# Feed-forward products of a decoder layer by a Strassen scheme, with the activations between them in DRAM

## The chip, the core and the metric

The kernel runs on one core of a Trainium2 chip. The metric is the device time of one execution in microseconds (us); the median of three runs is given. Matmuls run on TensorE (PE in the profile; PEld is its weight load), elementwise work on VectorE (DVE), ScalarE (ACT) and GpSimd (POOL); SyncE (SP) issues most DMAs.

## The reference

One post-norm layer on x of 1024 tokens by 1024 channels, all in float32:

```python
mixed = jnp.sum(gates * proj, axis=2) @ w_out[l]
x = _layer_norm(ALPHA * x + mixed, ln1_g[l], ln1_b[l])
hid = jax.nn.silu(x @ w_ffn_gate[l]) * (x @ w_ffn_up[l])
x = _layer_norm(ALPHA * x + hid @ w_ffn_down[l], ln2_g[l], ln2_b[l])
```

The three branches that make `proj` (a state-space branch, a gated recurrence and attention) are not touched. `w_ffn_gate` and `w_ffn_up` are 1024 x 2816, `w_ffn_down` is 2816 x 1024; 2816 are 22 blocks of 128.

## The kernel before

Each float32 product is made of three matmuls: every operand is split into a rounded part `hi` and a rest `lo`, and `mm3` (L108) adds hi·hi, hi·lo and lo·hi into one PSUM bank. `split` (L127) makes the parts: a copy on ACT that rounds, and a subtraction on DVE. A matmul has a stationary side of 128x128 and a moving side of 128x512.

The late part begins behind `merge(2)` (L950), which sums the branches into `mixed` and splits it.

- *Output projection.* `mix_out(tb, dh)` (L913) makes a block of 128 tokens by 512 channels with 24 matmuls; there are 16 such blocks, 384 matmuls. Its result is added to the input row (`stt`), `measure` (L894) takes bn_stats, and `norm` (L899) normalizes a block of 128 tokens: aggregate, square root on ACT, two multiplications, a reciprocal, two more.
- *Turning.* `turn_x(tb)` (L928) transposes a normalized block of tokens by 8 matmuls with the identity and splits it into `XH` and `XL`, the moving side of what follows.
- *Gate and up.* For each of 22 blocks `hb`, `hidden` (L967) sums gate and up for both halves of the tokens over 8 blocks of channels: four banks of 24 matmuls. Silu on ACT, the product of both on DVE, then a split.
- *Down.* The blocks `hb` are taken in chunks of three, the last of four (L978 to L980). Behind a chunk all 16 output blocks get its part (L998 to L1004) and are added in SBUF on DVE (L1008). Activations never leave SBUF. In the last chunk every block of tokens is normalized as soon as it is complete (L1012) and stored.

Weights come in 512 KB loads into `ws` (3 buffers), are split into `wh` and `wl` or into pairs of `m`. The late pools are `t` (9 large tiles and a few small ones, left side of SBUF) and `u` (15, right side). The framework's scheduler orders each engine's instructions with a time model; a tile pool makes an instruction wait until its buffer's last reader is done.

## Time and profile before

| | |
|---|---|
| runs shown | 1759.16 us median (1758.62 to 1762.29) |
| the profiled execution's own time | 1758.93 us |
| its span in the profile | 1757.2 us |
| PE busy | 1702.9 us, 97% of the span |
| DVE, ACT, POOL busy | 866.6, 532.5, 215.3 us |
| merge(2) ends, mix_out starts | 919.10 us |
| feed-forward starts | 1013.76 us |
| last matmul starts | 1748.05 us |

The profile is of one execution. The span runs from its first instruction to its last; the time of the run is 1.7 us longer. Starts are counted from the span's start. Matmuls are pipelined, so one matmul's duration (390 to 396 ns) is longer than the distance between two starts; the distance is what counts.

### The profile page before, as it was taken

What the parts mean: (1) busy time and instruction counts of PE and PEld (TensorE: products, weight loads), DVE (VectorE), ACT (ScalarE), POOL (GpSimd) and SP (SyncE); (2) the same over time, 40 slices, a digit from 0 to 9 for tenths busy, and PEclk for the clock granted to TensorE, in tenths of its full rate; (3) what the DMA queues carried; (4) which work ended last, traced back from release to release, by engine and by line L of the source; (5) the groups of instructions that cost most, each with busy time, mean ns of one, the idle gap of its engine ahead of it and who ended that gap; (6) DMA issues with size and microseconds to landing.
All of it is one profiled execution on the core that took longest, in us unless ns stands there. A gap on an engine that the chain in (4) does not pass through costs nothing.

```text
span 1757.2 us, 20254 instructions
## 1 busy us (share of the span) xinstructions
PE 1702.9 (97%) x7878; PEld 1399.6 (80%) x7878; DVE 866.6 (49%) x1648; ACT 532.5 (30%) x867; POOL 215.3 (12%) x285
## 2 busy tenths in 40 slices
PE   8989999999899998999999999999999999999998
PEld 6868877878688887888888888888888888888886
DVE  4756674624553468877486543232232323223238
ACT  4324454434443536552140131120202112020210
POOL 0210434214431021111400000000000000000000
PEclk9999999999899999999999999999999999999999
DMA  5342233233332434356673021120201111020102
GB/s 158 72 103 66 75 88 88 79 83 94 81 87 68 127 104 131 111 171 224 196 237 113 1 84 60 35 68 18 72 28 57 48 48 60 25 72 25 60 1 96
DMA packets 181789, 150.09 MB, mean 85 GB/s; under 512 B 29632, under 2 KB 153660, under 8 KB 181692
## 3 DMA queue, kind: packets, MB, share of 16 engines
q1 hardware_dynamic: 155580, 121.02, 23.7%
q10 hardware_dynamic: 26112, 27.76, 5.2%
q8 instruction: 62, 1.02, 0.2%
q14 instruction: 35, 0.29, 0.1%
HBM read 116.77 MB, written 31.98 MB: 85 GB/s over the span
## 4 chain that ended last, share of the span: by engine, by line
PE 80%; DMA 2%; DVE 2%; ACT 1%; POOL 1%; issue 1%; SPq 0%; ACTq 0%; DVEq 0%; POOLq 0%
PE b L106 49%; PE a L106 28%; PE s L106 1%; DMA nck<-ck_d 1%; PE a L330 1%; POOL s L114 1%; DMA s<-gl_d 1%; DMA nat<-s_c_re 0%; DVE s L114 0%; DVE x L122 0%; DVE wl L114 0%; DVE s L748 0%; DMA ws<-w_in 0%; POOL ndk L290 0%; PE b L933 0%
## 5 line engine op out<-in xcount | busy, mean ns | idle before, releaser
L106 PE MATMUL b<-x,wh 128*128 128x512 f32 x912 | 352.7, 398 | 2.5 <-ACT s L696 1.7
L106 PE MATMUL b<-x,wl 128*128 128x512 f32 x832 | 329.5, 396 | 0.0
L106 PE MATMUL b<-m,wh 128*128 128x512 f32 x784 | 310.4, 396 | 0.0
L114 DVE TENSOR_TENSOR wl<-ws,wh 128x1024 fp32r<-128x1024 f32 x106 | 136.7, 1290 | 142.7 <-ACT wh L128 132.6
L106 PEld LDWEIGHTS b<-x,wh 128*128 128x128 f32 x912 | 173.3, 190 | 37.6 <-ACT s L696 1.8
L128 ACT CAST wh<-ws 128x1024 fp32r<-128x1024 f32 x106 | 111.3, 1050 | 278.2 <-PE b L106 167.1
L106 PEld LDWEIGHTS b<-x,wl 128*128 128x128 f32 x832 | 158.2, 190 | 31.7
L106 PEld LDWEIGHTS b<-m,wh 128*128 128x128 f32 x784 | 149.3, 190 | 28.6 <-issue 0.2
L106 PE MATMUL b<-m,u 128*128 128x512 f32 x564 | 142.6, 396 | 0.0
L106 PE MATMUL a<-m,u 128*128 128x512 f32 x564 | 141.4, 396 | 0.0
L114 DVE TENSOR_TENSOR zs<-zs,a 128x512 f32<-128x512 f32 x44 | 30.3, 688 | 206.5 <-PE a L106 206.5
L106 PEld LDWEIGHTS a<-m,u 128*128 128x128 f32 x564 | 106.1, 188 | 25.5
L106 PEld LDWEIGHTS b<-m,u 128*128 128x128 f32 x564 | 106.0, 188 | 25.4
L106 PE MATMUL b<-u,wh 128*128 128x512 f32 x352 | 111.3, 396 | 0.0
L106 PE MATMUL a<-u,wh 128*128 128x512 f32 x352 | 111.1, 395 | 0.0
L106 PE MATMUL b<-t,wh 128*128 128x512 f32 x352 | 108.8, 390 | 0.0
L106 PE MATMUL a<-t,wh 128*128 128x512 f32 x352 | 108.7, 390 | 0.0
L114 POOL TENSOR_TENSOR s<-s,s 128x1024 f32<-128x1024 f32 (+9 forms) x76 | 78.5, 1034 | 209.1 <-ACT s L751 82.8
L128 ACT CAST m<-ws 128x1024 fp32r<-128x1024 f32 x26 | 27.4, 1055 | 248.1 <-PE a L106 186.7
L106 PEld LDWEIGHTS b<-u,wh 128*128 128x128 f32 x352 | 66.0, 188 | 16.4 <-DVE u L114 0.4
L106 PEld LDWEIGHTS a<-u,wh 128*128 128x128 f32 x352 | 66.0, 188 | 16.0
L106 PEld LDWEIGHTS b<-t,wh 128*128 128x128 f32 x352 | 66.0, 188 | 14.1
(256 smaller groups left out, 2631.8 us busy)
## 6 DMA issues: line engine op xcount, KB each, us to landing
ws<-w_in SPq DMA_DIRECT2D x48, 512.0 KB, 4.3
gate_d<-zs ACTq DMA_DIRECT2D x48, 256.0 KB, 2.1
zs<-gate_d SPq DMA_DIRECT2D x48, 256.0 KB, 3.3
ws<-w_ffn_gate SPq DMA_DIRECT2D x22, 512.0 KB, 3.8
ws<-w_ffn_up SPq DMA_DIRECT2D x22, 512.0 KB, 4.0
ws<-w_ffn_down SPq DMA_DIRECT2D x22, 512.0 KB, 3.2
ws<-w_branch SPq DMA_DIRECT2D x12, 512.0 KB, 5.6
s<-x SPq DMA_DIRECT2D x8, 512.0 KB, 7.1
```

The lines of the kernel that those rows point to most:

```text
L106: PE.matmul(o, a, b, start=first, stop=last)
L114: return e.tensor_tensor(o, a, b, op)
L128: ACT.copy(hi, src)
L330: PE.transpose(ta[:, j, e, :], pts[e][:, (k0 + j) * P : (k0 + j + 1) * P], ident)
```

## The change

*Gate and up.* The product is taken as a 2x2 matrix of quarters on one side (channels in two halves, gate and up as the two columns) and tokens in two halves on the other. A Strassen scheme in Winograd's form makes the four results from 7 products of quarters, 12 matmuls each, where 8 were needed. `turn` makes seven operands of x (`x11`, `x12`, `x22`, `s1` to `s4`) from both halves of the tokens, `sums` makes four sums of the weights of a block on POOL, and the products are combined by DVE additions (`begin`, `upper_gate`, `middle`, the loop). Blocks 0 to 2 take products 1 and 2 ahead of turn 7.

*Down.* The same scheme with pairs of blocks `hb` and halves of the output channels. For that the gated activations go to DRAM (`hid_d`), with their sums (`hids_d`, on POOL in `gated`) and the sums of the weights (`wts_d`, on POOL in `sums_down`). Then, product by product (order 1, 2, 6, 7, 5, 4), 11 steps each, `factors` loads two factors of 256 KB, splits them, and `blocks` runs 12 matmuls into four banks; `after_...` combines the banks with the residual. The factors of product 3 are all loaded and split ahead (22 tiles `p3`), so that it can be made one block of 128 tokens at a time with the normalization behind.

*Layout.* x behind the first normalization goes to DRAM (`x1_d`) and comes back as residual. The late pools are `keep`, `mid`, `right`, later `down`; PSUM is 8 equal banks. Small tiles of 4 bytes become 64, and an unused tile of 96 bytes lies at the right edge: in the built program before, the `u` tiles begin 32 bytes past a multiple of 64, and now every large tile begins on a multiple of 64. From turn 7 on, `pin` keeps DVE's, ACT's and POOL's instructions in the order of the program.

The core of the diff:

```diff
@@ -56,12 +56,16 @@
+    edge = ctx.enter_context(tc.tile_pool(name="edge", bufs=1, side="right"))
+    POOL.memset(edge.tile([P, 24], F32, name="edge"), 0.0)
...
-        "t": ("t", 9), "ln": ("t", 2), "u": ("u", 15),
+
+    LATE = {
+        "ws": ("keep", 4), "w": ("keep", 8), "x": ("keep", 9), "m8": ("mid", 4), "ln": ("mid", 2),
+        "mx": ("right", 8), "wo": ("right", 4), "r": ("down", 8), "row": ("down", 2), "p3": ("down", 22),
+    }
...
+    def pin(ins):
+
+        return tc.keep_in_program_order(ins) if pinned[0] else ins
+
     def tt(e, o, a, b, op):
-        return e.tensor_tensor(o, a, b, op)
+        return pin(e.tensor_tensor(o, a, b, op))
...
+    def operand(n, j, src, e):
+
+        if j == 0:
+            XO[n] = [new(HOME[n], F32R, (P, 4, 512)) for _ in range(2)]
+        hi, lo = [t[:, :, j * P : (j + 1) * P] for t in XO[n]]
+        ACT.copy(hi, src)
+        tt(e, lo, src, hi.bitcast(F32), ALU.subtract)
+
+    def turn(tb, place):
+        j = tb % 4
+        pa = []
         for q in range(2):
-            pa = bank([P, 4, P], "ba"[q])
+            pa.append(place(q))
             for k in range(4):
-                PE.transpose(pa[:, k, :], acc[tb][:, (4 * q + k) * P : (4 * q + k + 1) * P], ident)
...
+                PE.transpose(pa[q][:, k, :], acc[tb][:, (4 * q + k) * P : (4 * q + k + 1) * P], ident)
+        if tb < 4:
+            raw[j] = new("x", shape=(P, 8, P))
+            ACT.copy(raw[j][:, 0:4], pa[0])
+            DVE.tensor_copy(raw[j][:, 4:8], pa[1])
+            operand("x11", j, raw[j][:, 0:4], DVE)
+            operand("x12", j, raw[j][:, 4:8], POOL)
+            return
+        xs, s1 = new("x", shape=(P, 8, P)), new("x", shape=(P, 8, P))[:, 0:4]
+        x22, s2, s3, s4 = xs[:, 0:4], xs[:, 4:8], raw[j][:, 0:4], raw[j][:, 4:8]
+        ACT.copy(x22, pa[1])
+        tt(DVE, s3, s3, pa[0], ALU.subtract)
+        tt(DVE, s1, pa[0], x22, ALU.add)
+        tt(POOL, s2, x22, s3, ALU.subtract)
+        tt(POOL, s4, s4, s2, ALU.subtract)
+        operand("x22", j, x22, DVE)
+        operand("s3", j, s3, DVE)
+        operand("s2", j, s2, POOL)
+        operand("s1", j, s1, DVE)
+        operand("s4", j, s4, POOL)
...
+    def store_parts(hb, src, i, j):
+
+        hi, lo = [new("w", F32R, (P, 8, P)) for _ in range(2)]
+        split(src, hi, lo)
+        WT[hb][i], WT[hb][j] = [[t[:, c] for t in (hi, lo)] for c in (slice(0, 4), slice(4, 8))]
...
+    PRE = 3
+    for hb in range(PRE):
+        store_parts(hb, t, 1, 2)
...
+    def bank8(shape=(P, 512)):
+        return banks.tile(list(shape), F32, name=name("p"), tag="p", bufs=8)
...
+    def product(i, hb):
+        ps = bank8()
+        (wh_, wl_), (xh_, xl_) = WT[hb][i], XO[OF[i]]
+        for k in range(4):
+            mm3(ps, wh_[:, k], wl_[:, k], xh_[:, k], xl_[:, k], k == 0, k == 3)
+        return ps
+
+    def begin(hb):
+        ua, ub = new("x", shape=(P, 2, 512)), new("x", shape=(P, 2, 512))
+        G[hb] = dict(s1=ua[:, 0], u2=ua[:, 1], u3=ub[:, 0], gate=ub[:, 1])
+        pin(ACT.copy(G[hb]["s1"], product(1, hb)))
+
+    def upper_gate(hb):
+        g = G[hb]
+        tt(DVE, g["gate"], g["s1"], product(2, hb), ALU.add)
+        pin(ACT.activation(g["gate"], g["gate"], AF.Silu))
+    for hb in range(PRE):
+        begin(hb)
+        upper_gate(hb)
+    turn(7, lambda q: bank8([P, 4, P]))
+    pinned[0] = True
...
+    def sums(hb):
...
+        tt(POOL, t1, w12, w11, ALU.subtract)
+        tt(POOL, t2, w22, t1, ALU.subtract)
+        tt(POOL, t3, w22, w12, ALU.subtract)
+        tt(POOL, t4, w21, t2, ALU.subtract)
+
...
+    def parts_b(hb):
+        store_parts(hb, RAW[hb, 2][:, 0:8], 5, 6)
+        v = new("x", F32R, (P, 8, P))
+        split(RAW[hb, 1][:, 4:8], v[:, 0:4], v[:, 4:8])
+        WT[hb][3] = [v[:, 0:4], v[:, 4:8]]
+    def parts_c(hb):
+        store_parts(hb, RAW[hb, 2][:, 8:16], 7, 4)
...
+        tt(POOL, w11, w12, w11, ALU.subtract)
+        tt(POOL, w12, w22, w12, ALU.subtract)
+        tt(POOL, w22, w22, w11, ALU.subtract)
+        tt(POOL, w21, w21, w22, ALU.subtract)
+        for e, t in enumerate((wa, wb)):
+            SP.dma_start(wts_d[2 * j + e], t.rearrange("p a b -> p (a b)"))
...
+    def gated(hb):
+
+        g = G[hb]
+        t = hid[hb] = new("ln", shape=(P, 2, 512))
+        tt(POOL, t[:, 1], g["u3"], g["s1"], ALU.mult)
+        tt(POOL, t[:, 0], g["u2"], g["gate"], ALU.mult)
+        SP.dma_start(hid_d[hb], t.rearrange("p a b -> p (a b)"))
+        if hb % 2:
+            (x11, x21), (x12, x22) = [[t[:, 0], t[:, 1]] for t in hid[hb - 1 : hb + 1]]
+            tt(POOL, x11, x11, x21, ALU.subtract)
+            tt(POOL, x21, x21, x22, ALU.add)
+            tt(POOL, x22, x22, x11, ALU.subtract)
+            tt(POOL, x12, x12, x22, ALU.subtract)
+            for e in range(2):
+                SP.dma_start(hids_d[hb - 1 + e], hid[hb - 1 + e].rearrange("p a b -> p (a b)"))
+    sums(0)
+    parts_b(0)
+    parts_c(0)
+    sums(1)
+    middle(0)
+    for hb in range(NH):
+        g, more = G[hb], hb + 1 < NH
+        if hb + 2 < NH:
+            sums(hb + 2)
+        if hb % 2 == 0:
+            sums_down(hb // 2)
+        if more:
+            parts_a(hb + 1)
+        p5 = product(5, hb)
+        if more:
+            parts_b(hb + 1)
+        if hb >= PRE:
+            upper_gate(hb)
+        if more:
+            parts_c(hb + 1)
+        tt(DVE, g["s1"], g["u2"], product(7, hb), ALU.add)
+        tt(DVE, g["u3"], g["s1"], p5, ALU.add)
+        tt(DVE, g["u2"], g["u2"], p5, ALU.add)
+        if more:
+            if hb + 1 >= PRE:
+                begin(hb + 1)
+            middle(hb + 1)
+        tt(DVE, g["s1"], g["s1"], product(4, hb), ALU.add)
+        pin(ACT.activation(g["s1"], g["s1"], AF.Silu))
+        tt(DVE, g["u2"], g["u2"], product(3, hb), ALU.add)
+        gated(hb)
...
+    def factors(i, j, tag):
+        t = new("ws", shape=(P, 2, 512))
+        for e, (src, b, c) in enumerate(FACTORS[i]):
+            SP.dma_start(t[:, e], src[2 * j + b][:, c])
+        hi, lo = [new(tag, F32R, (P, 2, 512)) for _ in range(2)]
+        split(t, hi, lo)
+        return hi, lo
+    def blocks(Q, hl, first, last, tbs=range(4)):
+        hi, lo = hl
+        for tb in tbs:
             c = slice(tb * P, (tb + 1) * P)
+            mm3(Q[tb], hi[:, 0, c], lo[:, 0, c], hi[:, 1], lo[:, 1], first, last)
...
+    def settle(tb, dh, ps):
+        tt(DVE, res[tb][dh], res[tb][dh], ps, ALU.add)
+        pin(measure(res[tb][dh], tb, dh))
+    def finish(tb):
+        g2, b2 = rows_
+        norm(res[tb], tb, g2, b2, lambda dh: SP.dma_start(out[tb * P : (tb + 1) * P, 512 * dh : 512 * dh + 512], res[tb][dh]))
+    def after_5(Q):
+        for tb in range(4):
+            scaled(tb, 1, u2[tb])
+            tt(DVE, res[tb][1], res[tb][1], Q[tb], ALU.add)
+            residual(4 + tb)
             for dh in range(2):
...
+                scaled(4 + tb, dh, s1[tb])
+            settle(4 + tb, 1, Q[tb])
...
+    def after_4(Q):
+        for tb in range(4):
+            settle(4 + tb, 0, Q[tb])
+            finish(4 + tb)
+    steps = [(i, j) for i in (1, 2, 6, 7, 5, 4) for j in range(NJ)]
+    ends = {1: after_1, 2: after_2, 6: after_6, 7: after_7, 5: after_5, 4: after_4}
+    AHEAD = 3
+
+    def ready(n):
+        if n < len(steps):
+            pairs[steps[n]] = factors(*steps[n], "w")
+        elif n < len(steps) + NJ:
+            pairs[3, n - len(steps)] = factors(3, n - len(steps), "p3")
+    for n in range(AHEAD):
+        ready(n)
+    Q = None
+    for n, (i, j) in enumerate(steps):
+        if n >= len(steps) - NJ + 2:
+            ready(n + AHEAD + n - (len(steps) - NJ + 2))
+            ready(n + AHEAD + n - (len(steps) - NJ + 2) + 1)
+        else:
+            ready(n + AHEAD)
+        if j == 0:
+            Q = [bank8() for _ in range(4)]
+        blocks(Q, pairs.pop((i, j)), j == 0, j == NJ - 1)
+        if j == NJ - 1:
+            ends[i](Q)
+    Q = [bank8() for _ in range(4)]
+    for tb in range(4):
+        for j in range(NJ):
+            blocks(Q, pairs[3, j], j == 0, j == NJ - 1, [tb])
+        settle(tb, 1, Q[tb])
+        finish(tb)
```

**The order around turn 7.** On PE before (`u`, `t`: parts of x; `wh`, `wl`: of a weight; `ident`: transposes; `b`, `a`: PSUM):

```order
L106 MATMUL a_8918<-t_8548,wl_8912 128x512
L106 MATMUL a_8918<-t_8548,wh_8911 128x512
L106 MATMUL a_8918<-t_8549,wh_8911 128x512
L106 MATMUL a_8918<-t_8548,wl_8912 128x512
L933 MATMUL b_8972<-ident_72,x_8649 128x128 x4
L933 MATMUL a_8981<-ident_72,x_8649 128x128 x4
L106 MATMUL b_8990<-u_8846,wh_8905 128x512
L106 MATMUL a_8991<-u_8846,wh_8911 128x512
```

On PE now (`p`: PSUM; `mx`: operands of x; `w`: weights):

```order
L115 MATMUL p_9029<-mx_8560,w_8509 128x512
L115 MATMUL p_9029<-mx_8561,w_8509 128x512
L115 MATMUL p_9029<-mx_8560,w_8510 128x512
L984 MATMUL p_9044<-ident_77,x_8658 128x128 x4
L984 MATMUL p_9049<-ident_77,x_8658 128x128 x4
L115 MATMUL p_9096<-mx_8804,w_9078 128x512
L115 MATMUL p_9096<-mx_8805,w_9078 128x512
L115 MATMUL p_9127<-mx_8808,w_9078 128x512
L115 MATMUL p_9127<-mx_8809,w_9078 128x512
```

Behind the transposes of turn 7 stood products of another block's weights with x already turned; now product 5 of block 0 stands there (`mx_8804`, `mx_8805`: s1 in two parts, with the tokens of turn 7; `w_9078`, `w_9079`: parts of weight sums).

On POOL, which had nothing to do here before, at the same place (`x_9054`: x22 and s2, `x_8698`: s3 and s4, `mx_8805` and `m_8813`: low parts, `m_9073`: weight sums of block 0):

```order
L127 TENSOR_TENSOR x_9054<-x_9054,x_8698 128x512
L127 TENSOR_TENSOR x_8698<-x_8698,x_9054 128x512
L127 TENSOR_TENSOR mx_8805<-x_9054,mx_8804 128x4x128
L127 TENSOR_TENSOR m_8813<-x_8698,m_8812 128x4x128
L127 TENSOR_TENSOR m_9073<-ws_9071,ws_8495 128x512
L127 TENSOR_TENSOR m_9073<-ws_9071,m_9073 128x512
L127 TENSOR_TENSOR m_9073<-ws_9071 128x512
L127 TENSOR_TENSOR m_9073<-ws_8495,m_9073 128x512
```

The four sums of block 0 stand behind the four operations of turn 7.

**The order behind products 5 and 4 of the down product.** On DVE now (`r`: residual rows, `p`: PSUM, `w` and `p3` with `ws`: splits, of which 8 and 11 stand in a row):

```order
L127 TENSOR_TENSOR r_13169<-r_13169,p_12945 128x512
L925 BN_STATS bn_13174<-r_13169 128x6
L135 SCALAR_TENSOR_TENSOR r_12496<-r_12496,x_12026 128x512
L127 TENSOR_TENSOR r_12496<-r_12496,p_12946 128x512
L135 SCALAR_TENSOR_TENSOR r_13178<-r_13178,x_12024 128x512 x2
L127 TENSOR_TENSOR r_13178<-r_13178,p_12946 128x512
L925 BN_STATS bn_13183<-r_13178 128x6
L127 TENSOR_TENSOR w_13193<-ws_13189,w_13192 128x1024
L127 TENSOR_TENSOR w_13216<-ws_13212,w_13215 128x1024
```

The splits for steps 58 to 65 stand behind all of after_5. Further on, where the splits end:

```order
L127 TENSOR_TENSOR p_13424<-ws_13420,p_13423 128x1024
L127 TENSOR_TENSOR p_13443<-ws_13439,p_13442 128x1024
L127 TENSOR_TENSOR r_13151<-r_13151,p_13196 128x512
L925 BN_STATS bn_13156<-r_13151 128x6
L930 BN_AGGR mv_13460<-bn_13156 128x2
L135 SCALAR_TENSOR_TENSOR r_13151<-r_13151,mv_13460,row_13185 128x512 x2
L934 RECIPROCAL rs_13461<-rs_13461 128x1
L135 SCALAR_TENSOR_TENSOR r_13151<-r_13151,rs_13461,row_13187 128x512 x2
L127 TENSOR_TENSOR r_13160<-r_13160,p_13197 128x512
```

On DVE before, the last two blocks of tokens (`x`: rows, `b`, `a`: PSUM):

```order
L897 BN_STATS bn_13107<-x_8601 128x6
L114 TENSOR_TENSOR x_8649<-x_8649,b_13135 128x512
L901 BN_AGGR mv_13124<-bn_13107 128x2
L897 BN_STATS bn_13149<-x_8649 128x6
L122 SCALAR_TENSOR_TENSOR x_8601<-x_8601,mv_13124,ln_12837 128x512 x2
L906 RECIPROCAL rs_13125<-rs_13125 128x1
L114 TENSOR_TENSOR x_8649<-x_8649,a_13151 128x512
L122 SCALAR_TENSOR_TENSOR x_8601<-x_8601,rs_13125,ln_12839 128x512 x2
L897 BN_STATS bn_13149<-x_8649 128x6
L901 BN_AGGR mv_13166<-bn_13149 128x2
```

Before, additions and normalizations of one block of tokens followed the matmuls of that block; now eight blocks of addition, statistics and normalization stand behind the last split, four for product 4 and four for product 3.

## Rows read from the trace of the kernel before

**Rows 1.** Page part 1: busy us (share of the span) and instructions of each engine.
```profile
PE 1702.9 (97%) x7878; PEld 1399.6 (80%) x7878; DVE 866.6 (49%) x1648; ACT 532.5 (30%) x867; POOL 215.3 (12%) x285
```

**Rows 2.** The chain of waits from 880 us on, summed by line.
```profile
by line: PE b L106 49.1%; PE a L106 48.8%; DVE x L122 0.5%; PE b L933 0.4%; PE a L933 0.4%; DVE x L114 0.2%; DVE bn L897 0.1%; DVEq L1024 0.1%; DVE mv L901 0.0%; DVE rs L906 0.0%; issue 0.0%
```

**Rows 3.** Table by stretch: PE, PEld, DVE, ACT, POOL busy, granted clock, DMA share, GB/s.
```profile
900.00:950.00 50.00, 50.00 (x219) 40.83 (x219) 33.36 (x47) 11.76 (x16) 0.00 (x0) 1.00 0.63 210
1100.00:1200.00 100.00, 100.00 (x433) 81.18 (x433) 29.86 (x37) 16.04 (x21) 0.00 (x0) 1.00 0.16 48
```

**Rows 4.** PE timeline at the borders: start, duration (us), line, output <- inputs, count.
```profile
919.10 5.06 PE L106 MATMUL b<-u,t 128*128 128x512 f32 x21
...
1011.22 0.60 PE L933 MATMUL b<-ident,x 128*128 128x128 f32 x4
...
1013.76 0.71 PE L106 MATMUL b<-t,wh 128*128 128x512 f32 x2
...
1748.05 0.40 PE L106 MATMUL a<-m,t 128*128 128x512 f32 x1
```

**Rows 5.** PE timeline around 1137 us, with a u tile and without.
```profile
1132.41 0.63 PE L106 MATMUL a<-u,wh 128*128 128x512 f32 x2
...
1137.32 0.63 PE L106 MATMUL b<-t,wh 128*128 128x512 f32 x2
...
1138.47 0.63 PE L106 MATMUL b<-t,wh 128*128 128x512 f32 x2
...
1143.25 0.61 PE L106 MATMUL a<-t,wh 128*128 128x512 f32 x2
```

**Rows 6.** Groups of instructions from 1000 us on, DVE and ACT: busy, mean ns.
```profile
L114 DVE TENSOR_TENSOR wl<-ws,wh 128x1024 fp32r<-128x1024 f32 x42 | 51.5, 1226 | 89.4 <-ACT wh L128 86.5
...
L114 DVE TENSOR_TENSOR u<-zs,u 128x512 fp32r<-128x512 f32 x42 | 28.9, 688 | 13.8 <-ACT u L128 13.8
...
L128 ACT CAST wh<-ws 128x1024 fp32r<-128x1024 f32 x42 | 44.1, 1050 | 161.4 <-issue 82.2 <-PE b L106 79.2
L128 ACT CAST u<-zs 128x512 fp32r<-128x512 f32 x44 | 27.4, 622 | 120.8 <-DVE zs L114 120.8
```

**Rows 7.** Timeline of POOL and DVE between 845 and 857 us.
```profile
845.84 1.22 DVE L114 TENSOR_TENSOR wl<-ws,wh 128x1024 fp32r<-128x1024 f32 x1
846.00 3.46 POOL L114 TENSOR_TENSOR m<-m,zs 128x512 f32<-128x512 f32 x2 [3.52 <-DVE zs L122]
...
851.67 2.53 POOL L114 TENSOR_TENSOR m<-m,zs 128x512 f32<-128x512 f32 x2 [2.20 <-DVE zs L122]
...
854.84 1.28 POOL L114 TENSOR_TENSOR m<-m,zs 128x512 f32<-128x512 f32 x1 [0.65 <-DVE zs L122]
854.88 2.32 DVE L114 TENSOR_TENSOR wl<-ws,wh 128x1024 fp32r<-128x1024 f32 x1
```

**Rows 8.** PE timeline and table by stretch behind a PE stall (columns as in rows 3).
```profile
467.51 0.80 PE L106 MATMUL s<-q,q 128*128 128x256 f32 x2 [5.31 <-DVE st L307]
...
471.01 0.63 PE L106 MATMUL b<-x,wh 128*128 128x512 f32 x1
471.43 0.63 PE L106 MATMUL b<-m,wh 128*128 128x512 f32 x1
...
460.00:473.70 13.70, 7.88 (x22) 6.14 (x23) 6.98 (x20) 2.25 (x8) 7.43 (x9) 0.50 0.51 85
```

**Rows 9.** Page part 6, DMA issues: count, KB each, us to landing.
```profile
ws<-w_ffn_down SPq DMA_DIRECT2D x22, 512.0 KB, 3.2
```

**Rows 10.** DVE timeline at the end.
```profile
1748.48 0.69 DVE L114 TENSOR_TENSOR x<-x,a 128x512 f32<-128x512 f32 x1
1749.09 1.41 DVE L122 SCALAR_TENSOR_TENSOR x<-x,rs,ln 128x512 f32<-128x512 f32 x2
1750.41 0.68 DVE L897 BATCH_NORM_STATS2 bn<-x 128x6 f32<-128x512 f32 x1
...
1752.90 1.41 DVE L122 SCALAR_TENSOR_TENSOR x<-x,rs,ln 128x512 f32<-128x512 f32 x2
```

243 lines of the change are left out of this document (137 added, 106 removed).

## The prediction

> **What bounds the kernel now.** I read the page's busy times first. TensorE (PE) is busy 97% of the span, VectorE (DVE) 49%, ScalarE (ACT) 30% and GpSimd (POOL) 12% [rows 1]: PE is the candidate. The chain of waits from 880 us to the end settles it, since almost all of it lies on the matmuls of L106 [rows 2]; in this part no other engine ever ends a wait that matters. So the time of this part is a count of matmuls times their pace. The table by stretch gives the pace: 433 matmuls in a full 100 us, 231 ns each, at granted clock 1.00, while DVE works 29.9 us of the hundred, POOL nothing, and DMA is at 48 GB/s [rows 3]. The PE timeline gives the borders: the output projection (mix_out) starts at 919.10, the feed-forward at 1013.76 and the last matmul at 1748.05 [rows 4]. 3168 matmuls and one turn in 734.3 us are again 231.5 ns.
>
> The pace has two levels. Matmuls that read a u tile run 21 in 1132.41 to 1137.32, 233.8 ns each; those that read t, wh and wl run 21 in 1138.47 to 1143.25, 227.6 ns [rows 5]. In the built program the u tiles begin 32 bytes past a multiple of 64 and every other large tile on a multiple of 64; no other difference between these operands shows.
>
> **The change, part by part.** Up to the end of merge(2) every engine's order stays as it was, so PE reaches mix_out at 919.1 as now.
>
> *Fewer matmuls.* Gate and up: 7 products of 12 for 4 sums of 24 in each of 22 blocks, 1848 for 2112. Down: 77 steps of 12, 924 for 1056. 396 fewer at 231.5 ns are 91.7 us.
>
> *Pace.* In the changed program every large tile begins on a multiple of 64. I take 227.6 ns for all; the other end is 233.8. At the old pace of 231.5 the 2772 left would take 10.8 us more, and mix_out's 384 (all with u now) gain 2.4 us.
>
> *mix_out and turns.* 384 x 0.2276 = 87.4 us, and seven turns at 0.85 (three turns fill 1011.22 to 1013.76, [rows 4]) 6.0. New here is that turn 4 onward makes seven operands, four of the operations for each tile on POOL. POOL is in order and turn 6 waits for the normalization before it: from both sides 0 (hidden by mix_out) to 6 us (two POOL pairs at 1.27 and a split late), I take 3. First feed-forward product: 919.1 + 87.4 + 6.0 + 3 = 1015.5.
>
> *The fill behind turn 7.* PE has six products without sums (72 matmuls, 16.4 us) and then the eight transposes of turn 7. After these nothing is ready: an ACT copy (0.6), then on POOL, in the order shown, s2, s4, their two low parts and t1, t2 of sums(0), six operations at 1.27 [rows 7], then the cast (1.05) and the DVE split (1.23) [rows 6]. Bare, that is 0.6 + 7.6 + 1.05 = 9.3 until the first matmul and 10.5 until the first low part. Collisions (below) make it up to 15; with 1 us for the next block's sums I take 12. A stall of 5.3 us was followed by matmuls 427 ns apart at granted clock 0.50, the level of 1.2 GHz; twelve of them cost 12 x 0.2 = 2.4 more [rows 8]. The fill is 12 + 2.5, and the turn 0.9.
>
> *Steady first half.* A block has 84 matmuls, 19.1 us. DVE has three splits of 1.23, one of 0.69 and eight additions of 0.69, 9.9 us; ACT three casts of 1.05 and four short operations of 0.62, 5.6 us [rows 6]; both hide. POOL, idle here before, gets 20 operations of 128x512 in two blocks (8 sums of gate and up, 4 of down, 8 for gating and its sums): 20 x 1.27 = 25.4 of 38.2 us. POOL and DVE get in each other's way: a DVE split that began at 854.88 under a POOL operation took 2.32 for 1.23, and two POOL operations begun under a split 3.46 for 2.53 [rows 7]. If one waits for the other whenever both read two SBUF tensors, POOL's 25.4 and DVE's 2 x 4.4 add to 34.2 of 38.2 us: tight, but it fits. I cost it at nothing; the cover is those 4 us.
>
> The Trainium skill speaks against the change here (SBUF — State Buffer, "Who interferes with whom"): a VectorE instruction with two SBUF inputs and a GpSimd instruction that reads SBUF exclude each other for the whole instruction. The two rows agree (1.09 us of waiting and 0.93); by the rule alone the sum is that 34.2, so it still fits.
>
> DMA per block: 1 MB of gate and up loaded, 512 KB of down loaded and its sums written back, 512 KB of activations and of their sums written, 3 MB in 19.1 us, 160 GB/s; 210 GB/s moved between 900 and 950 with PE at full pace [rows 3]. Nothing. End of the first half: 1015.5 + 1848 x 0.2276 + 0.9 + 12 + 2.5 = 1451.5.
>
> *Second half.* Each step is 12 matmuls, 2.73 us, for 512 KB loaded (192 GB/s; a load of 512 KB lands in 3.2 us [rows 9], several are under way), a cast of 1.05 and a split of 1.23. That holds, with less room than any stage before. The first split queues behind the last additions: 0 to 3, I take 1.5. The 5 MB of residual rows loaded within steps 10 to 14: 0 to 4, I take 0, since three steps are prepared. After 55 steps (products 1, 2, 6, 7, 5): 1451.5 + 1.5 + 55 x 2.73 = 1603.2. Call this T5.
>
> Behind product 5 DVE must do 23 operations of about 0.67 (an addition moves on after 0.61, statistics take 0.68 [rows 10]), 15.4 us, ahead of the split of step 58 in its order. PE has steps 55 to 57 prepared, 8.2 us, so it waits some 7.6 us, and 2.5 more at half clock. That is not in the sum by itself, since the end lies on DVE: behind these 23 stand 19 splits. The last of them needs staging tiles, four in turn (a load of 3.2, a cast of 1.05, a split of 1.23 and the issue, about 6.5 us for four, 1.63 each): 15.4 + 19 x 1.63, about T5 + 47 to 50. Only then come, in DVE's order, eight blocks of addition, statistics and normalization. One takes 4.42 us now (the addition at 1748.48 to the pair at 1752.90 [rows 10]): 8 x 4.42 = 35.4. PE by then is done at T5 + 8.2 + 10 + 8 x 2.73 + 132 x 0.2276, about T5 + 70. So the tail changes hands: DVE ends at T5 + 48 + 35.4 = T5 + 83.4, 13 us after PE, where it now ends 6 us after. Bounds: T5 + 76, if only PE and one block count, and T5 + 92, if every split waits for a load.
>
> *Sum.* 1603.2 + 83.4 = 1686.6, and 2.9 from the last DVE operation to the span's end (1754.31 to 1757.2) gives a span of 1689.5. The profiled run's time was 1758.93 for 1757.2; its 1.7 gives 1691. The median shown is 1759.16, 0.2 above that run, which I neglect. Against 1758.9: 91.7 + 10.8 + 2.4 saved, about 37 given back.
>
> **The rivals.**
> A. *The pace does not improve.* Operands now come from other pools and the activations are themselves the stationary side; if 32 bytes are not the reason, matmuls stay at 231 to 234. For it: no row shows a u tile on a multiple of 64. Against: every t tile runs at 227.6 with the same partners. FFN1 and 55 steps of FFN2 are 2508 matmuls, x 3.9 to 6.2 ns = 10 to 16 us, mix_out 2: about 1705.
> B. *A feed runs short.* A step of 2.73 us needs its load, cast and split in time from four staging tiles; at 3.0 us a step 55 steps are 15 us longer; POOL a little behind in some blocks adds the same again: 1705 to 1740. For it: 34.2 of 38.2, and 192 GB/s through a whole stage, which no stretch of the trace sustains for so long. Against: 210 and 216 GB/s for 50 to 100 us around 900.
> C. *The waits are hidden better than I count.* If the fill is 9, turn 6 free and the last normalizations overlap the splits, PE alone bounds it: 919.1 + 87.4 + 6.0 + 0.9 + 2772 x 0.2276 + 9 + 4.4 + 2.9 + 1.7, about 1662, up to 1680.
> D. *Slower than before: POOL becomes the bound.* If each POOL operation meets a split and takes 1.28 + 0.93 = 2.21, 20 of them are 44.2 us and with 2 for the in-order wait on gated() 46 for 38.2: 7.9 x 11 pairs = 87 us, about 1778. It decides from a mean of 38.2/20 = 1.91 us for an operation. For it: POOL is in order and products 3 to 7 all need its sums. Against: splits fill 8.7 of 38.2 us, so most operations meet none.
>
> **How the numbers follow.** Forecast (1680 to 1700) 0.50, A 0.12, B 0.18, C 0.14, D 0.06. The range 1672 to 1716 takes the forecast, A, half of C and half of B, near 0.8. About 0.2% (3.5 us) is what a measurement of this kernel can tell from no change. Faster is everything but D and a sliver at the end of B: 0.93; within 0.2% 0.02; slower 0.05.
>
> **What would show it.** Right: 1848 and 924 matmuls in the two halves; 227 to 228 ns for all of them; one PE wait of 10 to 15 us behind turn 7, and one of 6 to 9 us near step 58, each followed by granted clock 0.50; POOL busy about 70% in the first half without ending a PE wait there; the last 35 us on DVE alone. Wrong: 231 ns or more (A); PE waits for POOL or for splits in every block (B, D); or a DVE that ends within 8 us of PE (C).

## The result and the profile after

The changed kernel took 1704.44 us, the median of 4 runs (1699.94 to 1705.95), and the kernel before 1758.89 us beside it (1757.67 to 1762.29). The ratio is 0.9683 with a 95% interval of 0.966 to 0.9706: faster by 3.2%. The forecast was 1691 with a range of 1672 to 1716. The sign and the range were right; the median came out 13 us later.

The profiled execution took 1699.94 us for a span of 1698.2. It is the fastest of the four, and the reason is ahead of the change: it reached mix_out at 913.91, 5.2 us sooner than the kernel before [rows 4], though every engine's order up to there is the same. Later kernels of this study with the same front reached that point at 917.2 to 922.7. In the traces it goes with the clock: ahead of mix_out, stretches at granted clock 0.50 add up to 23.9 us in this profile, to 34.1 in that of the kernel before, and to 27 to 38 in the later ones. So the 5.2 us are scatter, and the table counts from the start of mix_out.

| us from the start of mix_out | forecast | measured | more in this part |
|---|---|---|---|
| first feed-forward product | 96.4 | 100.9 | +4.5 |
| end of the first half (22 blocks) | 532.4 | 541.7 | +4.8 |
| product 5 done (T5) | 684.1 | 695.5 | +2.1 |
| last DVE operation | 767.5 | 781.1 | +2.2 |
| end of the span | 770.4 | 784.3 | +0.3 |

Together the parts are 13.9 us late. With the front of the kernel before, at 919.1, the span would have been 1703.4 and the time 1705.1, close to the median of 1704.44.

The page's first part, of the kernel after; PE has 396 matmuls fewer than in [rows 1], and POOL more than twice its busy time:

```profile
PE 1602.6 (94%) x7482; PEld 1324.8 (78%) x7482; DVE 1037.2 (61%) x1741; ACT 625.8 (37%) x952; POOL 592.5 (35%) x526
```

The table by stretch, with the columns of [rows 3]: the fill, a hundred microseconds of the first half, the wait near step 58, and the tail.

```profile
1013.00:1050.00 37.00, 25.24 (x100) 20.28 (x99) 25.16 (x28) 14.54 (x24) 18.87 (x13) 0.79 0.19 65
1100.00:1200.00 100.00, 100.00 (x443) 82.81 (x442) 55.81 (x59) 28.09 (x37) 85.69 (x55) 1.00 0.52 170
1600.00:1650.00 50.00, 42.10 (x180) 34.42 (x179) 36.08 (x42) 18.08 (x18) 0.00 (x0) 0.93 0.53 174
1650.00:1698.20 48.20, 28.88 (x128) 23.59 (x126) 41.96 (x70) 8.53 (x14) 0.00 (x0) 0.85 0.34 121
```

The second row stands against the row of the same stretch in [rows 3]: 443 matmuls now for 433, still without a gap, while POOL is busy 85.7 of the hundred and DMA moves 170 GB/s for 48. Only the other three stretches have idle time on PE.

What PE waited for from mix_out to the end (line, releaser, then us in total, times, longest):

```profile
PE p L115 <- ACT w L141: 14.2, 4, 11.1
PE p L115 <- DVE w L127: 10.4, 4, 7.9
PE b L984 <- issue: 5.8, 1, 5.8
```

The single waits in PE's timeline, with turn 6 at 1012.40, the fill behind turn 7 at 1045.12, and step 58 at 1626.44:

```profile
1012.40 1.09 PE L984 MATMUL b<-ident,x 128*128 128x128 f32 x4 [5.79 <-issue]
...
1014.86 18.25 PE L115 MATMUL p<-mx,w 128*128 128x512 f32 x72
...
1045.12 7.60 PE L115 MATMUL p<-mx,w 128*128 128x512 f32 x24 [11.13 <-ACT w L141]
...
1068.43 2.60 PE L115 MATMUL p<-wo,w 128*128 128x512 f32 x10 [1.28 <-DVE w L127]
1073.14 1.22 PE L115 MATMUL p<-mx,w 128*128 128x512 f32 x2 [2.11 <-ACT w L141]
...
1626.44 3.45 PE L115 MATMUL p<-w,w 128*128 128x512 f32 x8 [7.90 <-DVE w L127]
```

The first eight matmuls at 1626.44 lie 0.43 us apart, at granted clock 0.50, as the forecast had taken from [rows 8]. No row between 1075 and 1455 has a wait.

The end of DVE's timeline: the last split of product 3, the first two and the end of the eight blocks of addition, statistics and normalization.

```profile
1657.43 1.23 DVE L127 TENSOR_TENSOR p<-ws,p 128x1024 fp32r<-128x1024 f32 x1 [0.36 <-ACT p L141]
1658.58 0.68 DVE L127 TENSOR_TENSOR r<-r,p 128x512 f32<-128x512 f32 x1
...
1663.12 0.68 DVE L127 TENSOR_TENSOR r<-r,p 128x512 f32<-128x512 f32 x1
...
1693.59 1.42 DVE L135 SCALAR_TENSOR_TENSOR r<-r,rs,row 128x512 f32<-128x512 f32 x2
```

One block takes 4.54 us (1658.58 to 1663.12). PE's last matmul is at 1678.5, and DVE works on alone to 1695.0.

### The profile page after: what moved, and what is told of

It reads as the page before. It is cut to its first block, busy times and chain, and to the rows that moved or that the text cites. A ratio compares the mean times of both kernels' runs of the same rounds, so it can differ in the third digit from the quotient of the medians.

```text
span 1698.2 us, 20641 instructions
## 1 busy us (share of the span) xinstructions
PE 1602.6 (94%) x7482; PEld 1324.8 (78%) x7482; DVE 1037.2 (61%) x1741; ACT 625.8 (37%) x952; POOL 592.5 (35%) x526
## 4 chain that ended last, share of the span: by engine, by line
PE 66%; DVE 8%; DMA 5%; POOL 3%; issue 2%; ACT 2%; SPq 0%; ACTq 0%; DVEq 0%; POOLq 0%
PE p L115 30%; PE b L115 26%; PE a L115 7%; DMA ws<-w_ffn_down 2%; DVE r L135 2%; DMA nck<-ck_d 2%; PE s L115 1%; POOL m L127 1%; POOL s L127 1%; DVE s L127 1%; DVE r L127 1%; PE a L343 1%; DVE bn L925 1%; DMA s<-gl_d 1%; POOL x L127 1%
## 5 line engine op out<-in xcount | busy, mean ns | idle before, releaser
L115 PE MATMUL p<-mx,w 128*128 128x512 f32 x1056 | 251.5, 394 | 13.3 <-ACT w L141 13.2
L115 PEld LDWEIGHTS p<-mx,w 128*128 128x128 f32 x1056 | 200.7, 190 | 56.3 <-ACT w L141 14.4
L127 DVE TENSOR_TENSOR x<-x,p 128x512 f32<-128x512 f32 x163 | 108.4, 683 | 109.4 <-PE p L115 106.4
L115 PE MATMUL p<-w,w 128*128 128x512 f32 x528 | 156.6, 393 | 9.2 <-DVE w L127 9.1
L127 DVE TENSOR_TENSOR w<-ws,w 128x1024 fp32r<-128x1024 f32 x88 | 115.0, 1317 | 70.7 <-ACT w L141 70.1
L141 ACT CAST w<-ws 128x1024 fp32r<-128x1024 f32 x88 | 92.0, 1049 | 122.4 <-PE p L115 65.1
L115 PE MATMUL p<-wo,w 128*128 128x512 f32 x528 | 128.3, 392 | 1.3 <-DVE w L127 1.3
L115 PEld LDWEIGHTS p<-w,w 128*128 128x128 f32 x528 | 99.7, 190 | 32.0 <-DVE w L127 11.4
L115 PEld LDWEIGHTS p<-wo,w 128*128 128x128 f32 x528 | 99.9, 189 | 22.7 <-DVE w L127 1.7
L115 PE MATMUL p<-w 128*128 128x512 f32 x264 | 95.1, 390 | 0.9 <-ACT w L141 0.9
```

What stands on the lines that cost most here:

```text
L115: PE.matmul(o, a, b, start=first, stop=last)
L127: return pin(e.tensor_tensor(o, a, b, op))
L141: pin(ACT.copy(hi, src))
```

## Experiments

Each kernel of the study is given by its median and by its ratio to the kernel before, which ran beside it; where a few microseconds matter, the profiles are compared too, stage by stage from the start of mix_out. The profiles of the changed kernel, e7 and e8, whose programs agree up to there, put the end of the first half at 541.7, 541.5 and 541.9, so in that part a difference of 2 us can be read from a trace.

### What sets the pace: two changes of address, and one more

The forecast for the pace was right (227.6 ns, measured 226.7), but its reason, a tile that begins 32 bytes past a multiple of 64, needed a test. The first kernel moves the u tiles of the kernel before onto multiples of 64; the second moves mx and wo of the changed kernel to 32 past one.

```diff
 # e1, on the kernel before
+    edge = ctx.enter_context(tc.tile_pool(name="edge", bufs=1, side="right"))
+    POOL.memset(edge.tile([P, 24], F32, name="edge"), 0.0)
-    eps_t = small([P, 1], name_="eps")
+    eps_t = small([P, 16], name_="eps")[:, 0:1]
...
 # e2, on the changed kernel
+    shift = late_stack.enter_context(tc.tile_pool(name="shift", bufs=1, side="right", reuse_waits="tile"))
+    POOL.memset(shift.tile([P, 8], F32, name="shift"), 0.0)
```

> The kernel before with the padding of the change alone: small tiles of 64 bytes and an unused tile of 96 bytes at the right edge, so that the u tiles begin on a multiple of 64; every engine's order stays. Theory (the start of a tile sets the pace): the matmuls with a u tile go from 233.5 to 227 ns, about 2264 of them between 919 and 1748 us, 6.5 ns each, 14 to 15 us shorter, so 1744 us and a ratio of 0.992. Rival (the pace comes from something else in the changed kernel, such as its shorter products or its pools): u tiles stay at 233 and the time stays within 3 us of 1759. The changed kernel reached the output projection 5.2 us earlier than the kernel before; if that comes from the attention's tiles that the padding moves too, this run has it as well, if it is chance of loads in the first part, not.

> The changed kernel with an unused tile of 32 bytes ahead of its right-hand late pool, so that the operands of x (mx and wo, all but s4) begin 32 bytes past a multiple of 64; nothing else moves. Theory (start of a tile): the 384 matmuls of the output projection and the 1584 of products 1, 2, 4, 5, 6, 7 of the first half go from 227 to 233.5 ns, 1968 x 6.5 ns = 12.8 us longer, 1717 us; product 3 and the second half stay at 227. Rival (pace from elsewhere): all stay at 227 and the time within 3 us of 1704.

e1 measured 1758.99 us, ratio 0.9995 (0.9982 to 1.0007): nothing gained. The u matmuls keep their 233 ns on a multiple of 64, so that reason falls. e2 measured 1719.75, ratio 0.9783 (0.9766 to 0.9799), about 15 us over the changed kernel. In its PE timeline the matmuls with one shifted operand are slow, and in mix_out those with two are not (a `wo` tile and an `mx` tile, both shifted, against `m` and `mx`):

```profile
937.52 5.60 PE L115 MATMUL a<-wo,mx 128*128 128x512 f32 x24
942.96 5.77 PE L115 MATMUL b<-m,mx 128*128 128x512 f32 x24
...
1106.55 5.76 PE L115 MATMUL p<-mx,w 128*128 128x512 f32 x24
1112.15 2.96 PE L115 MATMUL p<-wo,w 128*128 128x512 f32 x12
...
1123.35 2.91 PE L115 MATMUL p<-m,x 128*128 128x512 f32 x12
1126.09 5.76 PE L115 MATMUL p<-mx,w 128*128 128x512 f32 x24
```

24 of mx from 1106.55 to 1112.15 are 233.3 ns each; 12 with m and x from 1123.35 to 1126.09 are 228. 24 with wo and mx from 937.52 to 942.96 are 226.7, though both begin 32 past a multiple of 64. So of the 384 of mix_out only half are slow, which the expectation had all slow; with the 1584 these 192 at 6.5 ns more are 11.5 us, and in the profile the end of the span, counted from mix_out, lies 11.1 us later. So an address does set the pace, but not by its place in 64 bytes.

Sorted by the two operands' start addresses in the built programs, all kernels so far fall in line in another way: a matmul of 128x512 runs at 227 ns where its stationary and its moving operand start at the same place modulo 256 bytes, and at 233 where they do not. From mix_out on, undisturbed distances between two starts are, in the kernel before, 227.6 on average for 1257 matmuls with no difference and 233.3 for 2280 with one; in e1 227.6 for 1257 and 233.1 for 2280 (there they were 128 apart); in the changed kernel 226.9 for all 3090, which agree; in e2 227.3 for 1349 and 233.4 for 1746. In the changed kernel 1738 of the 3090 are an odd multiple of 256 bytes apart and as fast as the rest. A fifth kernel tests it: before, with the *other* tiles moved, by 32 bytes. Now all of them lie 32 past a multiple of 64, which by the first reason makes everything slow.

```diff
-    eps_t = small([P, 1], name_="eps")
+    eps_t = small([P, 9], name_="eps")[:, 0:1]
```

> The kernel before with one small tile lengthened by 32 bytes, so that all tiles of the left side, too, begin 32 bytes past a multiple of 64, as the u tiles do; every order stays. In the runs so far matmuls took 227 to 228 ns wherever the starts of the moving and the stationary side were equal modulo 256 bytes, and 233 where they differ by 32, 128 or 224. Theory (the difference modulo 256 decides): here the difference is 0 for all matmuls of the late part, so the u pairs go from 233.4 to 227 though no tile begins on a multiple of 64: 2264 x 6 ns = 14 us less, 1745 us, ratio 0.992. Rival (a start off a multiple of 64 costs by itself): all matmuls go to 233, 8 to 10 us more from the late part alone, 1768 us or more.

It measured 1744.73 us, ratio 0.992 (0.9905 to 0.9935). The table by stretch, the kernel e5, as in [rows 3]:

```profile
1100.00:1200.00 100.00, 100.00 (x443) 82.81 (x442) 30.55 (x38) 16.02 (x21) 0.00 (x0) 1.00 0.16 48
```

It has the changed kernel's 443 matmuls where the kernel before has 433, by one padded constant. The u matmuls between these two rows of its PE timeline are 24 in 5.44 us, 226.7 each, against 233.8 in [rows 5]:

```profile
1123.54 0.62 PE L106 MATMUL b<-u,wh 128*128 128x512 f32 x2
...
1128.98 0.62 PE L106 MATMUL a<-u,wh 128*128 128x512 f32 x2
```

So of the 54 us about 14 are not Strassen's: they come from where the new pools put the tiles, and the kernel before can have nearly all of it.

### Is POOL near being the bound?

PE does not wait in the steady first half. Rival D said that it would. To see how far off it is, the four sums of gate and up are made twice, with the same result: 28 POOL operations in two blocks for 20.

```diff
-        tt(POOL, t1, w12, w11, ALU.subtract)
-        tt(POOL, t2, w22, t1, ALU.subtract)
-        tt(POOL, t3, w22, w12, ALU.subtract)
-        tt(POOL, t4, w21, t2, ALU.subtract)
+        for _ in range(2):
+            tt(POOL, t1, w12, w11, ALU.subtract)
+            tt(POOL, t2, w22, t1, ALU.subtract)
+            tt(POOL, t3, w22, w12, ALU.subtract)
+            tt(POOL, t4, w21, t2, ALU.subtract)
```

> The changed kernel with each of the four weight sums of every block done twice on POOL: 28 operations for two blocks instead of 20, the same result. Theory (POOL and DVE exclude each other where both read two SBUF tensors, so their times add): 28 x 1.27 + 8.7 = 44.3 us for two blocks against 38.1 us of matmuls, POOL becomes the bound, 6 us for each of some 10 pairs, 40 to 65 us more, about 1760, with PE waits on weight parts in every pair. Rival (they hardly cost each other, POOL needs only its own 28 x 1.27 = 35.6 us): below 38.1, so 0 to 6 us more, all of it in the fill.

It measured 1764.93 us, ratio 1.0034 (1.0015 to 1.0054): 60 us more, and 0.3% slower than the kernel before. Its PE waits between 1077 and 1518, the table by stretch, and PE's timeline there:

```profile
PE p L115 <- ACT w L141: 21.0, 14, 3.3
PE p L115 <- DVE w L127: 9.2, 18, 0.9
```

```profile
1200.00:1250.00 50.00, 47.57 (x206) 38.15 (x206) 22.66 (x24) 11.74 (x16) 48.58 (x33) 1.00 0.43 147
```

```profile
1256.70 4.14 PE L115 MATMUL p<-mx,w 128*128 128x512 f32 x10 [0.53 <-DVE w L127]
```

POOL is busy 48.6 of 50 us. The budget of the prediction says why: 28 x 1.27 = 35.5 and DVE's 8.8, if they exclude each other, are 44.3 for 38.1 us of PE's; with 20 operations they are 34.2, and PE never waits. The excess of 6.2 us for each of 11 pairs is 68; the run lost 60. By the distances between starts some 42 of these stand where PE waits (the lines above count only 30 as idle) and 13 in 66 more matmuls at half clock behind the waits (10 took 4.14 us at 1256.70). The mechanism of rival D is real, and by this budget the changed kernel has some 4 us in 38 to spare.

### The fill and turn 6

In the fill, ACT's cast and so PE wait for POOL. Of the kernel after, POOL's timeline there, and then DVE's ahead of turn 6, with pairs and splits of 2.80 to 3.41 us under POOL's operations:

```profile
1035.15 2.94 POOL L127 TENSOR_TENSOR x<-x,x 128x512 f32<-128x512 f32 x2 [12.26 <-ACT x L994]
1038.05 1.71 POOL L127 TENSOR_TENSOR mx<-x,mx 128x512 fp32r<-128x512 f32 x1
```

```profile
1004.50 2.80 DVE L135 SCALAR_TENSOR_TENSOR x<-x,mv,ln 128x512 f32<-128x512 f32 x2
1007.22 3.41 DVE L127 TENSOR_TENSOR wo<-x,wo 128x512 fp32r<-128x512 f32 x2
...
1010.74 3.23 DVE L135 SCALAR_TENSOR_TENSOR x<-x,rs,ln 128x512 f32<-128x512 f32 x2
```

Turn 6's wait has no releaser in the profile ("issue"), but its first four transposes start at 1012.40, when the first of the last two operations has ended (1012.30), and its other four wait until 1014.12, when the second has (1013.97). Behind turn 6, POOL idles 12.26 us before its first operation. Two edits use that time: one moves the sums of block 0 ahead of turn 7, one moves their cast and split there too.

```diff
-    turn(7, lambda q: bank8([P, 4, P]))
-    pinned[0] = True
...
     sums(0)
+    turn(7, lambda q: bank8([P, 4, P]))    # e3: here
+    pinned[0] = True
     parts_b(0)
+    turn(7, lambda q: bank8([P, 4, P]))    # e9: here instead
+    pinned[0] = True
     parts_c(0)
```

> The changed kernel with the weight sums of block 0 (four POOL operations and the load of its up weights) ahead of turn 7; the parts are split behind it as now. Theory (the fill is one chain: ACT copy, four POOL operations of the turn, two of the sums, cast, split): the sums leave the chain, PE waits for s1 and the split only, some 4 us in place of 11.1, and for POOL no more than 3 us later on; with one collision more ahead of turn 6 it saves 6 to 10 us, about 1696. Rival (the fill waits for the turn's own POOL operations or for a load anyway): the wait moves by less than 3 us and the time stays at 1704; or the sums collide with the splits ahead of turn 6 and the wait there grows by what is saved.

> The changed kernel with the weight sums of block 0 and, other than in the run before, also their cast and split ahead of turn 7. With the sums alone moved, PE still waited 7.2 us, and then 1.4. Theory (what is left is ACT's order: the cast of block 0's weight parts stands behind the cast of s4, which waits for two POOL operations of the turn): with the cast ahead of it PE waits only for s1 of turn 7, a copy, an addition, a cast and a split, some 4 us, and the time falls to about 1696. Rival (s1 itself is late, since its split stands behind others on DVE that POOL holds up): the wait stays at 6 us or more and the time at 1700.

e3 measured 1700.04 us, ratio 0.9669 (0.9654 to 0.9683). The wait of 11.13 became 7.15, and the start of the second half came 5.7 us sooner, counted from mix_out. e9 measured 1701.6, ratio 0.9669 (0.9653 to 0.9684), with 7.1 us sooner in the profile. Of its PE waits between 1000 and 1100, those behind turn 7:

```profile
PE p L115 <- ACT mx L975: 4.4, 1, 4.4
PE p L115 <- POOL mx L127: 2.2, 1, 2.2
PE p L115 <- ACT w L141: 2.1, 1, 2.1
```

What is late now is the operands that turn 7 itself makes: another releaser, a smaller wait. Both medians lie 3 to 4 us below the changed kernel's, short of the 1696 expected, and the intervals of the ratios overlap, so for each alone it is the trace that shows the gain.

For turn 6 two edits give PE the sum-free products of two blocks ahead of it. In e4 they use the eight new PSUM banks, in e10 the old pool's six.

```diff
-        if j:
+        if j in (1, 2):
             turn(3 + j, old)
...
         upper_gate(hb)
+        if hb == 1:
+            turn(6, lambda q: bank8([P, 4, P]))    # e4
+            turn(6, old)    # e10, and the pool of banks is opened behind it
```

> The changed kernel with products 1 and 2 of blocks 0 and 1 (48 matmuls, 10.9 us) ahead of turn 6 instead of behind it. Theory (turn 6 waits 5.8 us for a normalization that POOL operations stretch): the wait of 5.8 and 0.6 us and the 2 us at half clock behind it vanish, and with 24 matmuls left ahead of turn 7, whose normalization ends 6 us after that of turn 6, PE waits there for 0 to 3 us: 5 to 8 us less, about 1698. Rival (the same work only comes later): turn 7 waits by what turn 6 waited less and the time stays within 2 us of 1704.

> The changed kernel with products 1 and 2 of blocks 0 and 1 ahead of turn 6, now in the banks of the old PSUM pool; when they were moved with the new pool, PE waited 8.1 us for the last reader of the old pool's banks. Theory (that wait was the new pool's, and the normalization before turn 6 is what stretches the 5.8 us of the changed kernel): the 48 matmuls run at once, turn 6 finds its rows ready, and 5 to 8 us are saved, about 1698. Rival (the products' banks, too, wait for DVE, which is behind): PE waits 4 us or more at the first product and the time stays within 3 us of 1704.

e4 measured 1709.17 us, ratio 0.9721 (0.9703 to 0.9739), its median 5 us above the changed kernel's; from mix_out its second half starts 2.2 us later. PE's timeline of e4:

```profile
1020.52 12.72 PE L115 MATMUL p<-mx,w 128*128 128x512 f32 x48 [8.09 <-DVE x L135]
```

The products moved ahead had to wait as well. In the built program the first tile of the new pool lies on bank 0, and the last reader of bank 0 in the old pool is DVE's addition of mix_out's last block (`x<-x,a`, 1019.70 to 1020.37), which stands behind a normalization. e10 goes round this and measured 1704.22, ratio 0.9687 (0.9671 to 0.9703), as long as the changed kernel by the medians; from mix_out its second half starts 3.8 us sooner and its span ends 1.2 us sooner. Turn 6's wait of 5.8 us is gone, and behind it stands another of 4.03, with ACT's copy that ends it:

```profile
1027.37 0.57 ACT L994 COPY x<-a 128x512 f32<-128x512 f32 x1
1027.99 8.47 PE L115 MATMUL p<-mx,w 128*128 128x512 f32 x24 [4.03 <-ACT x L994]
```

This is the wait of e4 once more. The 24 are block 2's, the first in the new pool, and so on bank 0 again; here its last user is turn 6 (`a`), which that copy reads. The old pool has banks 0 to 5, so 6 and 7 lay idle, but no kernel was run that begins there or keeps block 2 in the old banks.

### Step 58 and the tail

The forecast has PE waiting 7.6 us near step 58 and the end on DVE regardless. Two edits take these apart. e8 spreads the 23 DVE operations behind product 5 over the steps of product 4, so that PE need not wait; DVE's total work stays. e7 prepares the factors of product 3 earlier, one in four steps from step 15 on, so that splits leave DVE's queue near the end.

```diff
 # e8
-    def after_5(Q):
-        for tb in range(4):
+    def after_5(Q, tbs=range(4)):
+        for tb in tbs:
...
+        if i == 4 and j in (2, 4, 6):
+            after_5(Q5, [j // 2])
...
 # e7
-        if n >= len(steps) - NJ + 2:
-            ready(n + AHEAD + n - (len(steps) - NJ + 2))
-            ready(n + AHEAD + n - (len(steps) - NJ + 2) + 1)
-        else:
-            ready(n + AHEAD)
+        ready(n + AHEAD if n + AHEAD < len(steps) else len(steps) + NJ)
+        if n >= 15 and n % 4 == 3 and (n - 15) // 4 < NJ:
+            ready(len(steps) + (n - 15) // 4)
```

> The changed kernel with the 24 DVE operations behind product 5 cut into four groups, one behind the product and one at steps 57, 59 and 61 of the next. Theory (the PE wait of 7.9 us at step 58 is the split queued behind these operations, but the end stands on DVE, whose work stays the same): the wait falls to 0 to 2 us and PE ends 8 to 10 us sooner, while the time falls by no more than 4 us, 1700 to 1704. Rival (the wait at step 58 counts in full): 8 to 10 us less, about 1695.

> The changed kernel with the factors of product 3 loaded and split one in four steps from step 15 on, instead of two a step behind product 5; so the normalizations of tokens 4 to 7 no longer stand behind eleven of these splits. Theory (the tail is eight blocks of 4.54 us on DVE that start only when the last split is done): the four blocks for product 4 start with its matmuls' end, some 9 us sooner, and the end moves by 7 to 10 us, about 1696; DVE then ends 5 to 8 us behind the last matmul; the wait of 7.9 us behind product 5 stays. Rival (the tail is set by PE, or the added loads, 240 GB/s, stall the steps): PE waits appear between steps 15 and 55 and the time stays within 3 us of 1704.

e8 measured 1703.64 us, ratio 0.9684 (0.9669 to 0.9699), the changed kernel's median within 1 us, though its PE does not wait at all there (the stretch 1600 to 1650 has PE busy 50.00 of 50.00, where the changed kernel has 42.10) and has its last matmul 9 us sooner from mix_out. DVE's eight blocks still begin only after the last split:

```profile
1662.36 1.22 DVE L127 TENSOR_TENSOR p<-ws,p 128x1024 fp32r<-128x1024 f32 x1 [0.51 <-ACT p L141]
1663.50 0.68 DVE L127 TENSOR_TENSOR r<-r,p 128x512 f32<-128x512 f32 x1
```

The last split ends 45.1 us behind product 5, where it was 49.3: DVE has the same 43 operations in that stretch, 38 us of work in both, and idles 7.5 us for 11.2. The span ends 84.6 us behind product 5, for 88.9 in the changed kernel and 90.4 to 91.3 in e3, e4, e9 and e10, whose tail is the same. So PE is done 9 us sooner, and the end gets 4 to 7 us of that by the traces, as DVE's operations fill the gaps between the splits, and next to nothing by the medians, whose runs lie up to 4.5 us from them. The four runs do not settle which. e7 measured 1695.38, ratio 0.9645 (0.963 to 0.9659), 7 to 9 us better. Now DVE waits for PE, in its timeline:

```profile
1657.51 0.69 DVE L127 TENSOR_TENSOR r<-r,p 128x512 f32<-128x512 f32 x1 [6.53 <-PE p L115]
```

The 6.53 us came because the scheduler, with product 3's factors at hand, put 59 of its matmuls among those of product 4, whose end the eight blocks wait for. That also filled the wait at step 58, which the expectation had left in place, and DVE ends 18 us behind the last matmul, not 5 to 8.

### All together

e11 joins e9, e7 and e8, and pins PE's program order from product 4 on, so that the interleaving of e7 goes. e12 adds e10's edit of turn 6. The only lines that are not above:

```diff
-        PE.matmul(o, a, b, start=first, stop=last)
+        ins = PE.matmul(o, a, b, start=first, stop=last)
+        if pinned[-1] == "PE":
+            tc.keep_in_program_order(ins)
...
+        if i == 4 and j == 0:
+            pinned.append("PE")
```

> The changed kernel with three edits at once: block 0's sums and split ahead of turn 7, product 3's factors prepared one in four steps from step 15 on, the operations behind product 5 cut into four groups; and PE's order from product 4 on kept as written, so that all of product 4 stands ahead of product 3. Theory (each wait has its own cause, so the gains add): 4 to 7 us at the fill; with the step 58 wait gone product 4 ends 30 us behind product 5 and the eight blocks of 4.54 us begin there, so DVE ends 67 us behind product 5, where it was 86: 18 us less; in all 1678 to 1684. Rival (the splits of product 4 and the four groups together are more than DVE does in time: 24 x 0.67 + 8 x 1.23 = 26 us of 30): PE waits in product 4, half of the gain at the end is lost, 1688 to 1694.

> The kernel with these three edits and also products 1 and 2 of blocks 0 and 1 ahead of turn 6, in the old pool's banks. Theory (in the run of that edit alone the wait at turn 6 was gone, but a wait of 4.0 us for the copy behind it had come, since ACT and DVE are behind there by what POOL holds up): 2 to 4 us less than with the three edits, 1675 to 1681. Rival (DVE sets the end of this stretch whatever PE does first, so the fill behind turn 7 grows by as much): no difference from the three edits within 1.5 us.

e11 measured 1679.27 us, ratio 0.9549 (0.9536 to 0.9562); it beats both kernels, the changed one by 25 us. e12 measured 1680.01, ratio 0.9555 (0.9542 to 0.9568): no difference by the medians. The PE waits from mix_out to the end, of e11 and then of e12:

```profile
PE b L986 <- issue: 5.8, 1, 5.8
PE p L115 <- ACT mx L977: 4.5, 1, 4.5
PE p L115 <- ACT w L143: 3.2, 3, 2.1
PE p L115 <- DVE w L129: 2.0, 3, 1.0
PE p L115 <- POOL mx L129: 1.9, 1, 1.9
PE a L986 <- DVE x L137: 0.6, 1, 0.6
```

```profile
PE p L115 <- ACT x L996: 7.9, 1, 7.9
PE p L115 <- ACT mx L977: 3.1, 1, 3.1
PE p L115 <- ACT w L143: 3.0, 3, 2.0
PE p L115 <- POOL mx L129: 2.2, 1, 2.2
PE p L115 <- DVE w L129: 1.9, 2, 1.0
```

Turn 6's 5.8 and 0.6 are gone in e12, and a wait of 7.9 is there instead: 18.0 us in all for e11, 18.1 for e12. It is e10's wait for turn 6's copy on bank 0, longer because that copy ends only at 1034.92 here. Counted from mix_out, e12's second half all the same starts 2.5 us sooner and its span ends 2.4 us sooner, in one profile of each; its front took 2.5 us longer than e11's in these profiles. So the edit's 2 to 4 us are neither shown nor refuted by the times, and whether PE would stand without the wait for bank 0 was not tried. e11's tail, in the table by stretch:

```profile
1600.00:1640.00 40.00, 40.00 (x178) 33.14 (x177) 32.77 (x40) 15.85 (x15) 0.00 (x0) 1.00 0.45 148
1640.00:1674.00 34.00, 30.81 (x136) 25.16 (x135) 32.88 (x61) 2.36 (x8) 0.00 (x0) 1.00 0.29 108
```

PE is full up to 1640, and DVE is busy 32.9 of the 34 us behind it: what bounds the end now is the eight blocks, some 36 us from when the first of them can start.

## Why the prediction was right, and 13 us short

- **Fewer matmuls, and their pace.** Right in size: 396 matmuls are gone, and all the others run at 226.7 ns (forecast 227.6). The reason given for the pace was wrong: not 32 bytes past a multiple of 64 (e1), but a difference between the starts of the two operands (e5). The step held by luck, because in the changed kernel both things are true at once. mix_out gained 1.4 us, not 2.4: its matmuls had not all been slow, but 230.7 ns apart on average.
- **Rival A** has the time that was measured, 1705, and is refuted all the same: its pace of 231 to 234 appears in no stretch. Two causes gave one number, and only the table by stretch tells them apart.
- **Turn 6**, forecast at 3 us between bounds of 0 and 6, is the first term that was too small. PE stood 5.8 us and once more 0.6, and the transposes ran at half clock (four took 1.09 us for 0.60), 7.9 in all. The pairs of normalizations ahead of it took 2.80 and 3.23 us under POOL's operations, for 1.41 in [rows 10]. The upper bound had two POOL pairs at their undisturbed 1.27.
- **The fill**, forecast at 15.4 us with the turn and the half clock, was 21.9. Its first wait was right, 11.1 for 12 less 1. What was missing are the places where the first two blocks catch up (1.28 and 2.11 us at 1068 and 1073), half clock again behind them, and the eight slow matmuls that turn 6 handed on. e9 shows that it is a matter of order: with the sums and their cast done in POOL's idle 12 us, the second half starts 7.1 us sooner.
- **The steady first half** was costed at nothing and cost nothing. The 4 us of cover were the number to check, and e6 took them away: beyond 38 us the two engines' sum appears in PE's waits. Of VectorE's splits, all with two SBUF inputs, two of three took 1.68 us on average there and one 1.38, for 1.23 in [rows 6], the short one 1.78 for 0.69, and POOL's operations 1.59 for 1.27, without a wait on PE. That agrees with the rule of the Trainium skill that the prediction weighed (SBUF — State Buffer, "Who interferes with whom"). With the longer operations POOL is busy 86% of the time, where the forecast had 70.
- **The second half** took 4.2 us beyond 660 matmuls at 226.7 ns, for 1.5. Of these 1.3 is the wait at its start, and some 2.7 stand between 1492 and 1528, where the residual rows are loaded; the forecast had bounded it by 0 and 4 and taken 0.
- **Step 58 and the tail** were right in mechanism and nearly in size: a PE wait of 7.9 (forecast 7.6), the last split at T5 + 49.3 (47 to 50), the last DVE operation at T5 + 85.6 (83.4), 16 us behind PE. Blocks took 4.54 us for 4.42. e8 bears out by its median the claim that the PE wait is not in the sum, while its trace has 4 to 7 us of it there, since the 23 operations behind product 5 hold up the splits; e7 shows that the splits are in the sum. The sign "the last 35 us on DVE alone" did not fit the forecast's own 13 us, nor the measured 16; the eight blocks take 36.
- **Rival B** (a feed runs short) did not happen: steps of 12 matmuls ran in 2.72 us but for those small waits. **Rival C** (1662 to 1680) is not what this kernel does, but what it becomes once its three holes are closed: e11's 1679.

So the terms that were too small lie at the borders of the stages, where POOL and DVE meet: turn 6 was priced from durations that each engine has when the other is idle, and the fill without the places where the first blocks catch up and the half clock behind them. They make 9.3 of the 13.9 us, what the pace gave back already taken off; the second half and the tail share the rest. How much of turn 6's wait is POOL's and how much DVE's own order was not tried.

## What to carry to other kernels

A matmul count gives the big term, but what is given back lies at the borders of stages, where operands are made by an in-order chain over several engines: price such a chain with the durations that its engines have together, and add the half-clock matmuls behind each hole. Before removing a wait, find which engine ends last behind it; closing a PE wait of 7.9 us hardly moved the median while DVE's queue set the end, and splits moved out of that queue were worth 7 to 9. Where a new PSUM pool follows an old one, see whose bank its first tile gets. Look at the pace itself, too: lay out both operands of a matmul so that their starts agree modulo 256 bytes, and compare the same operation on different tiles to see whether they do.
